# Adding the forget gates' running sums by the score product, as rows beside the keys' low halves

## The chip, the cores and the metric

The kernel runs on one core of a Trainium2 chip. The metric is the device time of one execution in microseconds (us). Three runs of the kernel before gave 1219.63, 1219.83 and 1220.3 us; the median is 1219.83.

## What is computed

Two layers, each of an attention part and a feed-forward part, over 512 tokens of 1024 numbers. The attention part has three groups of four heads: "fox" (a causal softmax with a bias from forget gates), "diff" (two score maps a head) and "mla". The change is in the fox heads:

```python
def fox_group(q, k, v, f_logit, f_bias):          # 4 heads of 64
    logf = log_sigmoid(f_logit + f_bias)
    cum = cumsum(logf, axis=1).transpose(0, 2, 1)  # one running sum a head
    def bias(qi, ki):
        d = cum[query] - cum[key]
        return where(ki <= qi, d, -1e30)
    return softmax(q @ k.T * 64 ** -0.5 + bias) @ v
...
for each layer:
    h = rmsnorm(x) @ w_in          # split into q, k, v, gates of all heads
    x = x + concat(fox, diff, mla) @ w_o
    up = conv(rmsnorm(x) @ w_up);  x = x + (silu(g) * u) @ w_down
```

All is float32. The kernel keeps that precision by splitting a number into a high and a low half of TensorE's faster float type and multiplying three times (high by high, high by low, low by high).

## The kernel before, in words

Each layer has these stages. First, products that give tokens in rows: the gates and fox values (`w_fx`), then the diff values (`w_dv`), with two projections between (`fm(0)` and `fm(2)`, the first two fox queries and keys). Then the "weave": the twelve heads, two at a time, are interleaved with the remaining projections and with the output product, which fill TensorE while a head waits for its softmax. These fillers are the groups of `mm` products of 128x512. Last, the feed-forward part, nothing but large products.

A fox head keeps queries as one tile whose upper 64 partitions hold one head's high half and whose other 64 hold its low half. The keys are a tile `k` (the high half twice) and a tile `lo` (the low half in the head's own 64 partitions, zeros in the other 64). Scores are two products with the same `q`: `q` by `k`, then `q` by `lo`.

A head is a job of steps: four scores `s(3)`, `s(2)`, `s(1)`, `s(0)` of 512, 384, 256 and 128 columns, transposes `t(kt)` of the weight rows, and products `v(kt)` with the values into the tile `o`. `soft` is one VectorE instruction that adds the bias to the scores and takes the minimum (`nm`), then an exponential on ScalarE, then a reciprocal (`rsum`) on VectorE; `plain` scales the row on GpSimd; `transposed` turns the row on TensorE (tile `at`) and splits it into `ph` and `pl`.

The biases of a fox head come from `prep`. The running sums stand in `cum`, one column for each block and head. Four transposes by the identity (`at<-c_sb,cum`) spread a head's sums over all partitions, ScalarE copies them negated (`r`), VectorE makes the masked blocks (`r<-c_sb,at`), and GpSimd adds the query's own sum into four bias tiles `b` (seven instructions). Heads 0 and 1 do this before the weave, heads 2 and 3 as a step of heads 0 and 1, in line before `t(1)`.

The order on every engine is made when the program is built: a table of costs in `Plan` estimates when a tile is ready, `weave` takes a head's step if it is ready by then and a filler otherwise, and a scheduler below it orders each engine's own queue. Engines work in order, each through its own queue. All compute instructions carry one line of the program, L135 (a helper that records them), so groups are told apart by tile names.

Of the kernel before, what the change touches and what calls it, by code (L numbers as in the profile page):

```python
# [14 lines left out]
P = 128  # L15
# [19 lines left out]
NPAR = DEPTH * PL  # L35


C_ID, C_TRI, C_ONE, C_CAU, C_COS, C_SIN, C_MLA, C_ALI = 0, 128, 256, 384, 512, 576, 640, 1152
NCST = C_ALI + S

BIG = 3.0e38
HALVES = (slice(0, 64), slice(64, 128))
# [116 lines left out]
def constants():  # L159
    c = np.zeros((P, NCST), np.float32)  # L160
    p = np.arange(P)
    c[:, C_ID:C_ID + P] = np.eye(P)
    c[:, C_TRI:C_TRI + P] = np.where(p[:, None] <= p[None, :], 8.0, 0.0)
    c[:, C_ONE:C_ONE + P] = 8.0
    c[:, C_CAU:C_CAU + P] = np.where(p[None, :] <= p[:, None], 0.0, 8 * NEG)
# [12 lines left out]

def build(tc, xT, cst, par, lamv, w_fm, w_dv, w_fx, w_uq, w_ukv, w_o, w_o2, w_up, w_dn, w_dt, fin, out):
# [4 lines left out]
    with ctx:  # L184
# [23 lines left out]
        def U():  # L208
            return plan.tile("u", 2, up_.tile([P, S], F32, name="u", tag="u"))

        def B(qt):
            return plan.tile(f"b{qt}", 1, pp.tile([P, (qt + 1) * P], F32, name=f"b{qt}", tag=f"b{qt}"))
# [21 lines left out]
        g_sb = cp.tile([P, KD], F32, name="g_sb")  # L234
        par_sb = cp.tile([P, NPAR], F32, name="par_sb")
        mhalf = cp.tile([P, NT], F32, name="mhalf")
        ones = cp.tile([P, 2], F32, name="ones")

        nc.scalar.dma_start(g_sb, par[:, O_LN1:O_LN1 + KD])
# [1 line left out]
        nc.vector.memset(rest.bitcast(F32), 0.0)  # L241
        nc.gpsimd.memset(ones, 1.0)
        nc.gpsimd.memset(mhalf, -0.5)
        warm = small(2, "warm")
        nc.scalar.activation(warm, ones, AF.Copy)

# [224 lines left out]
                else:  # L471
                    assert not (jobs or side or fillers), "nothing can go on"

        def head_job(name, gates, maps, reads, bias_of, scale, v_mul, o_put, combine, prep=None):

            job = Job(name, gates)
            rows, pT, out = [None] * NT, {}, []

            def s(qt):
                def emit():  # L480
                    rs, ts = [], []
                    b = bias_of(qt)
                    for m in maps:
                        ps = m(qt)
                        t = row_tile(qt) if not ts else U()
                        rs.append(soft(ps, qt, t, b, scale))
                        ts.append(t)
                    combine(qt, ts, rs)
                    rows[qt] = ts[0]
                job.add(emit, lambda: (reads(), "sc"))  # L490

            def t(kt):
                def emit():
                    pT[kt] = transposed(rows, kt)
                job.add(emit, lambda: (rows[kt:], "at"))

            def v(kt):
                def emit():
# [6 lines left out]
            if prep:  # L505
                job.add(prep)
# [25 lines left out]
        def attention(l, norm):  # L532
# [19 lines left out]
            def stacked_queries(i, scale=1.0):  # L552

                yield from fm(i)
                t = got[i]
                got[i] = []
                for m in range(2):
                    q = A()
                    own, other = HALVES[m], HALVES[1 - m]
                    nc.scalar.activation(q[own], t[own], AF.Copy, scale=scale)  # L560
                    if scale == 1.0:
                        nc.vector.tensor_tensor(out=q[other], in0=t[own], in1=q[own].bitcast(F32), op=ALU.subtract)
                    else:
                        nc.vector.scalar_tensor_tensor(out=q[other], in0=t[own], scalar=scale, in1=q[own].bitcast(F32), op0=ALU.mult, op1=ALU.subtract)
                    got[i].append(q)
                yield f"fm{i}"

            def stacked_keys(i):

                yield from fm(i)  # L570
                t = got[i]
                got[i] = []
                for m in range(2):
                    k, lo = A(), A()
                    own, other = HALVES[m], HALVES[1 - m]
                    nc.gpsimd.memset(lo[other].bitcast(F32), 0.0)
# [3 lines left out]
                    got[i].append((k, lo))  # L580
                yield f"fm{i}"

            def stacked_tiles(iq, ik):
                return lambda: [*got[iq], *(t for pair in got[ik] for t in pair)]
# [41 lines left out]
            norm.spread()  # L626
            for _ in first:
                pass
            marks[f"fm{FM_ORDER[0]}"] = 0.0
# [9 lines left out]
            marks[f"fm{FM_ORDER[1]}"] = 0.0  # L639


            nz = NT * 4
# [16 lines left out]
            cum = small(nz, "cum")  # L659
            cum_ps = at_ps()  # L660

            def cumulate(k):
                if k != 5:
                    return
                nc.tensor.matmul(cum_ps[:, 0:nz], lhsT=c_sb[:, C_TRI:C_TRI + P], rhs=lf, start=True, stop=False)
                for t in range(1, NT):
                    nc.tensor.matmul(cum_ps[:, 4 * t:nz], lhsT=c_sb[:, C_ONE:C_ONE + P], rhs=lf[:, 0:nz - 4 * t], start=False, stop=t == NT - 1)
                nc.vector.tensor_copy(cum, cum_ps[:, 0:nz])

            def rotate(dst, src, cs, sn, shape, name):  # L670

# [18 lines left out]


            acc = tm(w_dv, S, (mm_ps, mm_ps, sc_ps, sc_ps), cumulate)
            dv = []
            for t in range(NT):
                dv.append(split(acc[t], scale=rs1[:, t:t + 1]))
# [101 lines left out]


            jobs = []
            box = {}  # L800
            preps = {}

            def plain(qt, ts, rs):
                n = (qt + 1) * P
# [26 lines left out]
            def fox(h):  # L831
                pair, par = divmod(h, 2)

                def bias(qt):
                    n = (qt + 1) * P
                    b = B(qt)
                    nck, msk = box[f"nck{h}"]
                    for src, c in ((nck, slice(0, n - P)), (msk, slice(n - P, n))):
                        if c.start < c.stop:
                            nc.gpsimd.tensor_scalar(out=b[:, c], in0=src[:, c], scalar1=1.0, scalar2=cum[:, 4 * qt + h:4 * qt + h + 1], op0=ALU.mult, op1=ALU.add)  # L840
                    box[f"b{h}_{qt}"] = b

                def prep():
                    ps = over_partitions([cum[:, 4 * t + h:4 * t + h + 1] for t in range(NT)])
                    nck, msk = R(), R()
                    nc.scalar.activation(nck, ps, AF.Copy, scale=-1.0)
                    for t in range(NT):
                        c = slice(t * P, (t + 1) * P)
                        nc.vector.tensor_tensor(out=msk[:, c], in0=c_sb[:, C_CAU:C_CAU + P], in1=ps[:, c], op=ALU.subtract)
                    box[f"nck{h}"] = nck, msk  # L850
                    for qt in reversed(range(NT)):
                        bias(qt)

                if h < 2:
                    prep()
                else:
                    preps[h - 2] = prep

                def bias_of(qt):
                    return box[f"b{h}_{qt}"]  # L860

                return head_job(f"fox{h}", [f"fm{pair}", f"fm{2 + pair}"],
                                [stacked_scores(pair, 2 + pair, par)], stacked_tiles(pair, 2 + pair), bias_of, 0.125,
                                halves_mul(lambda: fv, h), pair_put(f"f{pair}", par, pair), plain, lambda: preps[h]() if h in preps else None)

            def diff(h):
                def combine(qt, ts, rs):
# [217 lines left out]
```

## Time and profile before

| What | Before |
|---|---|
| median of three runs | 1219.83 us |
| the profiled execution, whole | 1220.15 us |
| its span, first to last instruction | 1218.3 us |
| granted TensorE clock, mean | 0.999 of full speed |
| TensorE busy | 1205.1 us (99%) |
| VectorE busy | 822.1 us (67%) |
| ScalarE busy | 661.9 us (54%) |
| GpSimd busy | 208.1 us (17%) |

TensorE's records overlap, so its cost is read from the distance between starts and not from the durations. The weave runs from about 54 to 260 us in the first layer and from about 654 to 860 us in the second; the two layers look alike.

### The profile page before, as it was taken

The numbers are of one execution on the slowest core, as the hardware profiler recorded it, in microseconds if no ns is written. First come the engines' busy times: TensorE is split into PE (matmuls) and PEld (weight loads), VectorE is DVE, ScalarE is ACT, GpSimd is POOL, SyncE is SP. The second block draws the span as 40 slices with busy tenths as digits, with TensorE's granted clock in tenths as the row PEclk, the third lists the DMA queues.
The fourth block names the chain that finished last, engine by engine and source line by source line (L and its number), as shares of the span: only waits on it lengthen the run. The fifth ranks groups of instructions, "written<-read, shape, count | busy, mean of one in ns | idle before, by whom it ended". The sixth has DMA issues, their size and how long they took to land.

```text
span 1218.3 us, 16462 instructions
## 1 busy us (share of the span) xinstructions
PE 1205.1 (99%) x5776; PEld 1005.2 (83%) x5776; DVE 822.1 (67%) x1691; ACT 661.9 (54%) x1323; POOL 208.1 (17%) x320
## 2 busy tenths in 40 slices
PE   9999999999999999999999999999999999999997
PEld 8888888888888888888888888888888888888886
DVE  6678888787674366765556888877767634676743
ACT  6577787555543245444455776866555422545424
POOL 0262432001110001010013415220111100101102
PEclk9999999999999999999999999999999999999999
DMA  6321111223323333223323211112332233232331
GB/s 230 113 70 48 57 53 40 88 86 105 103 81 86 113 103 103 99 72 95 90 101 104 70 66 49 40 49 88 100 102 100 72 100 112 102 100 91 102 106 69
DMA packets 34497, 108.31 MB, mean 89 GB/s; under 512 B 3952, under 2 KB 4080, under 8 KB 34416
## 3 DMA queue, kind: packets, MB, share of 16 engines
q1 hardware_dynamic: 33840, 106.45, 27.1%
q8 instruction: 45, 0.74, 0.3%
q10 hardware_dynamic: 576, 0.83, 0.2%
q14 instruction: 36, 0.29, 0.1%
HBM read 105.16 MB, written 2.10 MB: 88 GB/s over the span
## 4 chain that ended last, share of the span: by engine, by line
PE 93%; POOL 2%; DVE 2%; ACT 2%; issue 1%; DMA 0%; POOLq 0%; SPq 0%; ACTq 0%; DVEq 0%
PE mm L135 78%; PE sc L135 8%; PE at L135 4%; PE o L135 3%; POOL b L135 1%; DVE w L135 1%; ACT u L135 1%; ACT row L135 0%; POOL row L135 0%; DVE a L135 0%; DVE row L135 0%; DMA raw<-in_w_fx 0%; ACT a L135 0%; POOL rsd L135 0%; ACT w L135 0%
## 5 line engine op out<-in xcount | busy, mean ns | idle before, releaser
L135 PE MATMUL mm<-a,whi 128*128 128x512 f32 x2736 | 850.9, 392 | 0.0
L135 PEld LDWEIGHTS mm<-a,whi 128*128 128x128 f32 x2736 | 508.4, 188 | 101.8 <-DVE a L135 0.4
L135 PE MATMUL mm<-a,wlo 128*128 128x512 f32 x1368 | 533.2, 390 | 0.0
L135 ACT ACTIVATE whi<-raw 128x512 fp32r<-128x512 f32 (+3 forms) x426 | 248.0, 584 | 362.5 <-PE mm L135 323.8
L135 DVE TENSOR_TENSOR wlo<-raw,whi 128x512 fp32r<-128x512 f32 (+3 forms) x426 | 272.8, 641 | 126.8 <-ACT whi L135 122.0
L135 PEld LDWEIGHTS mm<-a,wlo 128*128 128x128 f32 x1368 | 256.8, 188 | 53.5
L135 DVE SCALAR_TENSOR_TENSOR w<-u,par_sb,w 128x510 f32<-128x510 f32 (+1 forms) x176 | 133.0, 761 | 28.0 <-ACT w L135 25.3
L135 POOL TENSOR_TENSOR a<-w,a 128x512 fp32r<-128x512 f32 x44 | 57.6, 1309 | 527.4 <-ACT a L135 508.1
L135 DVE TENSOR_TENSOR u<-mm,r 128x512 f32<-128x512 f32 x84 | 58.0, 691 | 98.9 <-PE mm L135 98.9
L135 ACT ACTIVATE a<-w 64x512 fp32r<-64x512 f32 (+1 forms) x124 | 78.3, 631 | 40.9 <-DVE w L135 39.5
L135 ACT ACTIVATE w<-u,par_sb 128x512 f32<-128x512 f32 x88 | 71.4, 815 | 29.4 <-DVE u L135 29.3
L135 POOL TENSOR_SCALAR row<-row,rsum 128x512 f32<-128x512 f32 (+1 forms) x96 | 57.4, 600 | 151.8 <-DVE rsum L135 144.1
L135 PE MATMUL sc<-a 128*128 128x512 f32 (+7 forms) x288 | 66.5, 338 | 1.6 <-DVE nm L135 1.6
L135 DVE TENSOR_TENSOR x<-mm,x 128x512 f32<-128x512 f32 x64 | 43.9, 688 | 34.0 <-PE mm L135 33.7
L135 ACT ACTIVATE row<-row,nm 128x512 f32<-128x512 f32 (+1 forms) x96 | 53.8, 561 | 18.3 <-DVE nm L135 17.9
L135 PEld LDWEIGHTS sc<-a 128*128 128x128 f32 (+1 forms) x288 | 45.4, 190 | 7.2 <-DVE nm L135 3.0
L135 DVE TENSOR_TENSOR pl<-at,ph 128x128 fp32r<-128x128 f32 (+1 forms) x96 | 45.7, 482 | 7.5 <-ACT ph L135 7.1
L135 ACT ACTIVATE ph<-at 128x128 fp32r<-128x128 f32 (+1 forms) x96 | 40.8, 433 | 14.0 <-PE at L135 8.7
L135 PE MATMUL mm<-whi,a 128*128 128x512 f32 (+2 forms) x144 | 46.7, 363 | 0.0
L135 PE MATMUL at<-c_sb,row 128*128 128x128 f32 x240 | 42.1, 276 | 0.9 <-POOL row L135 0.9
L135 POOL TENSOR_SCALAR b<-r,cum 128x128 f32<-128x128 f32 (+2 forms) x56 | 28.8, 527 | 63.4 <-ACT r L135 42.9
L135 ACT ACTIVATE w<-w 128x512 f32<-128x512 f32 x50 | 31.7, 634 | 14.4 <-DVE w L135 11.5
(156 smaller groups left out, 1072.9 us busy)
## 6 DMA issues: line engine op xcount, KB each, us to landing
raw<-in_w_up SPq DMA_DIRECT2D x88, 512.0 KB, 3.3
raw<-in_w_fm SPq DMA_DIRECT2D x30, 512.0 KB, 3.2
raw<-in_w_dn SPq DMA_DIRECT2D x24, 384.0 KB, 3.1
raw<-in_w_dn SPq DMA_DIRECT2D x24, 320.0 KB, 2.9
raw<-in_w_o SPq DMA_DIRECT2D x16, 384.0 KB, 3.1
raw<-in_w_dv SPq DMA_DIRECT2D x8, 512.0 KB, 3.3
raw<-in_w_dn SPq DMA_DIRECT2D x8, 512.0 KB, 3.5
raw<-in_w_o SPq DMA_DIRECT2D x4, 512.0 KB, 3.3
```

The costliest lines, as they stand in the source:

```text
L135: return real(*args, **kw)
```

## The change

The sums are no longer biases. `cumulate`, which runs inside the `w_dv` product, splits the sums into high and low halves of four heads (`hl`, eight numbers a token and block); GpSimd copies them into a mostly zero tile `gate_rows` at four places, and two steps later four transposes turn it, and ScalarE copies the result to `box["sums"]`, in which partitions now hold sums and columns hold tokens. `summed` writes such rows into the half of a 64-partition pair that held nothing: for keys into the zeros beside the low half in `lo`, with a minus sign and rows of ones; for queries into a new tile `q2`, whose other half is a copy of `q`'s. The second score product now is `q2` by `lo`, so the 64 idle rows of the product add the sums. The bias that `soft` adds is the constant causal mask.

```diff
+            def summed(i):
+                for m in range(2):
+                    own, other = HALVES[m], HALVES[1 - m]
+                    if i < 2:
+                        q = got[i][m]
+                        out, f = A(), C_SUM + 2 + 2 * (2 * i + m)
+                        nc.gpsimd.tensor_copy(out[own], q[own])
+                        got[i][m] = q, out
+                    else:
+                        out, f = got[i][m][1], C_SUM
+                    nc.gpsimd.tensor_scalar(out=out[other], in0=box["sums"][other], scalar1=c_sb[other, f:f + 1], scalar2=c_sb[other, f + 1:f + 2], op0=ALU.mult, op1=ALU.add)
...
+                    nc.tensor.matmul(ps[:, :n], lhsT=q[:, c], rhs=k[:, :n], start=True, stop=False)
+                    nc.tensor.matmul(ps[:, :n], lhsT=q2[:, c], rhs=lo[:, :n], start=False, stop=True)
...
             def cumulate(k):
+                if k == 7:
+                    ps = at_ps()
+                    for t in range(NT):
+                        nc.tensor.transpose(ps[:, t * P:(t + 1) * P], in_=gate_rows[:, t, :], identity=ident)
+                    box["sums"] = R()
+                    nc.scalar.activation(box["sums"], ps, AF.Copy)
                 if k != 5:
                     return
...
-                nc.vector.tensor_copy(cum, cum_ps[:, 0:nz])
+                nc.scalar.activation(hl[:, :, 0:4], src, AF.Copy)
+                nc.vector.tensor_tensor(out=hl[:, :, 4:8], in0=src, in1=hl[:, :, 0:4].bitcast(F32), op=ALU.subtract)
+                for c in (0, 8, 64, 72):
+                    nc.gpsimd.tensor_copy(gate_rows[:, :, c:c + 8], hl.bitcast(F32))
...
             acc = tm(w_dv, S, (mm_ps, mm_ps, sc_ps, sc_ps), cumulate)
+            for i in FM_ORDER[:2]:
+                summed(i)
...
-                def prep():
-                    ps = over_partitions([cum[:, 4 * t + h:4 * t + h + 1] for t in range(NT)])
-                    nck, msk = R(), R()
-                    nc.scalar.activation(nck, ps, AF.Copy, scale=-1.0)
-                    for t in range(NT):
-                        c = slice(t * P, (t + 1) * P)
-                        nc.vector.tensor_tensor(out=msk[:, c], in0=c_sb[:, C_CAU:C_CAU + P], in1=ps[:, c], op=ALU.subtract)
-                    box[f"nck{h}"] = nck, msk
-                    for qt in reversed(range(NT)):
-                        bias(qt)
```

`fm(1)` and `fm(3)` call `summed` at their ends; the zeroing of `lo` goes for fox keys; the table of constants grows from 1664 to 2058 columns.

The order moves with it. On TensorE, at the end of the `w_dv` product of the first layer and the start of the weave, `sc` being score tiles, `mm` the products and `at` the transposes, before:

```order
L135 MATMUL sc<-whi,a 128x512
L135 MATMUL at<-c_sb,cum 128x128 x8
L135 MATMUL mm<-a,whi 128x512 x2
L135 MATMUL mm<-a,wlo 128x512
...
L135 MATMUL mm<-a,whi 128x512 x2
L135 MATMUL mm<-a,wlo 128x512
L135 MATMUL sc<-a 128x512 x2
L135 MATMUL sc<-a 128x384 x2
```

And now, from the last twelve products of `w_dv` on:

```order
L137 MATMUL sc<-whi,a 128x512
L137 MATMUL at<-c_sb,gate_rows 128x128 x4
L137 MATMUL mm<-whi,a 128x512
...
L137 MATMUL mm<-a,whi 128x512 x2
L137 MATMUL mm<-a,wlo 128x512
L137 MATMUL sc<-a 128x512 x2
L137 MATMUL sc<-a 128x384 x2
```

The eight transposes after `w_dv` are gone, four stand twelve products before its end, and the first scores come after 18 filler products of 512 columns instead of 12.

On TensorE further on, between the last score of head 0 (128 columns) and the transpose of the row that it gives (`row_862` before, `row_858` now), before:

```order
L135 MATMUL sc<-a 128x128 x2
L135 MATMUL mm<-a,whi 128x512
L135 MATMUL at<-c_sb,cum 128x128 x4
L135 MATMUL mm<-a,whi 128x512
L135 MATMUL mm<-a,wlo 128x512
...
L135 MATMUL at<-c_sb,row_751 128x128
L135 MATMUL at<-c_sb,row_862 128x128
```

And now:

```order
L137 MATMUL sc<-a 128x128 x2
L137 MATMUL mm<-a,whi 128x512 x2
L137 MATMUL mm<-a,wlo 128x512
...
L137 MATMUL at<-c_sb,row_790 128x128
L137 MATMUL sc<-a 128x256 x2
L137 MATMUL mm<-a,whi 128x512 x2
...
L137 MATMUL at<-c_sb,row_858 128x128
```

The four transposes of the sums are gone, and 30 filler products stand between the two places instead of 12.

On GpSimd, from the weave's start on, where `b` are bias tiles, `r` the spread sums and `row` the softmax rows, before:

```order
L135 TENSOR_SCALAR b_721<-r,cum 128x128
L135 TENSOR_SCALAR row_751<-row_751,rsum 128x512
L135 TENSOR_SCALAR row_762<-row_762,rsum 128x384
L135 MEMSET a 64x512
L135 TENSOR_SCALAR row_789<-row_789,rsum 128x512
L135 TENSOR_SCALAR row_800<-row_800,rsum 128x384
L135 TENSOR_SCALAR b_724<-r,cum 128x128 x2
L135 TENSOR_SCALAR b_727<-r,cum 128x128
L135 TENSOR_SCALAR row_844<-row_844,rsum 128x256
L135 TENSOR_SCALAR b_882<-r,cum 128x384
L135 TENSOR_SCALAR b_885<-r,cum 128x256
L135 TENSOR_SCALAR row_862<-row_862,rsum 128x128
```

And now:

```order
L137 COPY a<-a 64x512 x2
L137 COPY gate_rows<-hl 128x4x8 x4
L137 TENSOR_SCALAR a<-r,c_sb 64x512 x4
L137 TENSOR_SCALAR row_735<-row_735,rsum 128x512
L137 TENSOR_SCALAR row_746<-row_746,rsum 128x384
L137 TENSOR_SCALAR a<-r,c_sb 64x512
L137 COPY a<-a 64x512 x2
L137 TENSOR_SCALAR a<-r,c_sb 64x512
L137 TENSOR_SCALAR row_790<-row_790,rsum 128x512
L137 TENSOR_SCALAR row_801<-row_801,rsum 128x384
L137 TENSOR_SCALAR a<-r,c_sb 64x512
L137 TENSOR_SCALAR row_840<-row_840,rsum 128x256
```

The `b` instructions between the rows are gone; fewer and wider ones that write the sums' rows stand between them, and none is left once `fm(3)` is done.

## Rows read from the trace of the kernel before

**Rows 1.** The page, busy time of the engines.

```profile
PE 1205.1 (99%) x5776; PEld 1005.2 (83%) x5776; DVE 822.1 (67%) x1691; ACT 661.9 (54%) x1323; POOL 208.1 (17%) x320
```

**Rows 2.** Waits of PE: line, waited for, us in total, times, longest.

```profile
PE sc L135 <- DVE nm L135: 1.6, 2, 0.8
...
PE at L135 <- POOL row L135: 0.9, 2, 0.4
PE at L135 <- DVE pl L135: 0.8, 2, 0.4
```

**Rows 3.** The chain of waits in time order: start, us, work.

```profile
89.99 4.13 PE mm L135 x18
```

**Rows 4.** Timeline of PE, heads 0 and 1: start, us, instruction, [idle before].

```profile
54.11 1.04 PE L135 MATMUL at<-c_sb,cum 128*128 128x128 f32 x8
54.90 0.70 PE L135 MATMUL mm<-a,whi 128*128 128x512 f32 x2
55.45 0.40 PE L135 MATMUL mm<-a,wlo 128*128 128x512 f32 x1
```

**Rows 5.** Timeline of PE, the sums of head 2.

```profile
65.58 0.44 PE L135 MATMUL mm<-a,whi 128*128 128x512 f32 x1
66.15 0.65 PE L135 MATMUL at<-c_sb,cum 128*128 128x128 f32 x4
66.56 0.48 PE L135 MATMUL mm<-a,whi 128*128 128x512 f32 x1
66.87 0.39 PE L135 MATMUL mm<-a,wlo 128*128 128x512 f32 x1
```

**Rows 6.** Timeline of PE, the sums of head 3.

```profile
76.68 0.62 PE L135 MATMUL at<-c_sb,cum 128*128 128x128 f32 x4
77.06 0.71 PE L135 MATMUL sc<-a 128*128 128x512 f32 x2
```

**Rows 7.** Timeline of PE, four transposes between products of another stage.

```profile
25.43 0.65 PE L135 MATMUL at<-c_sb,rsn 128*128 128x128 f32 x4
25.84 0.71 PE L135 MATMUL mm<-a,whi 128*128 128x512 f32 x2
26.39 0.40 PE L135 MATMUL mm<-a,wlo 128*128 128x512 f32 x1
```

**Rows 8.** Timeline of VectorE and PE around the running sums.

```profile
46.00 0.17 DVE L135 COPY cum<-at 128x16 f32<-128x16 f32 x1 [2.10 <-PE at L135]
...
51.39 0.39 PE L135 MATMUL mm<-whi,a 128*128 128x512 f32 x1
```

**Rows 9.** Groups by form: instruction, shapes, count, busy us, mean ns, idle before.

```profile
L135 POOL TENSOR_TENSOR a<-w,a 128x512 fp32r<-128x512 f32 x44 | 57.6, 1309 | 527.4 <-ACT a L135 508.1 <-issue 19.3
...
L135 POOL TENSOR_SCALAR row<-row,rsum 128x512 f32<-128x512 f32 x24 | 18.5, 771 | 43.8 <-DVE rsum L135 43.8
...
L135 POOL TENSOR_TENSOR rsn<-vn,mhalf 128x4 f32<-128x4 f32 x4 | 4.1, 1016 | 166.7 <-DVE vn L135 166.7
...
L135 POOL COPY w<-krr 128x128 f32<-128x128 f32 x8 | 2.2, 291 | 7.4 <-DVE a L135 7.4
```

**Rows 10.** The same groups, ScalarE.

```profile
L135 ACT ACTIVATE whi<-raw 128x512 fp32r<-128x512 f32 x278 | 174.5, 630 | 231.4 <-PE mm L135 194.0 <-PE sc L135 29.7 <-issue 1.9
```

**Rows 11.** The bias tiles' instructions: count, ns min/median/max, first and last start, forms.

```profile
L135 POOL TENSOR_SCALAR b<-r,cum x56: 370/380/990, 56.1 to 691.9; 128x128 f32<-128x128 f32 x40, 128x384 f32<-128x384 f32 x8, 128x256 f32<-128x256 f32 x8
```

**Rows 12.** Timeline of PE and GpSimd, the row of head 0's last score.

```profile
69.19 0.49 PE L135 MATMUL at<-c_sb,row 128*128 128x128 f32 x3
...
69.68 0.37 POOL L135 TENSOR_SCALAR row<-row,rsum 128x128 f32<-128x128 f32 x1
...
70.10 0.66 PE L135 MATMUL at<-c_sb,row 128*128 128x128 f32 x4 [0.43 <-POOL row L135]
```

**Rows 13.** Weight loads of one layer's score products: count, ns min/median/max, first and last start, forms.

```profile
L135 PEld LDWEIGHTS sc<-a x144: 186/190/212, 57.5 to 220.7; 128*128 128x128 f32 x96, 96*128 96x128 f32 x48
```

**Rows 14.** Windows: stretch, its us, busy us of PE, PEld, DVE, ACT, POOL, clock, DMA.

```profile
165.00:205.00 40.00, 39.39 (x232) 31.46 (x231) 35.97 (x109) 33.80 (x99) 9.59 (x17) 1.00 0.08 27
```

More of the change, by code (lines that the diff above doesn't have):

```diff
@@ L35 @@
 NPAR = DEPTH * PL
-C_ID, C_TRI, C_ONE, C_CAU, C_COS, C_SIN, C_MLA, C_ALI = 0, 128, 256, 384, 512, 576, 640, 1152
-NCST = C_ALI + S
+C_ID, C_TRI, C_ONE, C_COS, C_SIN, C_MLA, C_ALI, C_CAU = 0, 128, 256, 384, 448, 512, 1024, 1536
+C_SUM = C_CAU + S
+NCST = C_SUM + 10
 BIG = 3.0e38
@@ L164, in constants @@
     c[:, C_ONE:C_ONE + P] = 8.0
-    c[:, C_CAU:C_CAU + P] = np.where(p[None, :] <= p[:, None], 0.0, 8 * NEG)
+    c[:, C_CAU + S - P:C_CAU + S] = np.where(p[None, :] <= p[:, None], 0.0, 8 * NEG)
+    row = p % 64
+    first, second = row < 8, (row >= 8) & (row < 16)
+    c[:, C_SUM], c[:, C_SUM + 1] = -1.0 * first, second
+    for h in range(FOX_H):
+        own = row % FOX_H == h
+        c[:, C_SUM + 2 + 2 * h], c[:, C_SUM + 3 + 2 * h] = second & own, first & own
     half = ROPE // 2
@@ L209, in U @@
             return plan.tile("u", 2, up_.tile([P, S], F32, name="u", tag="u"))
-        def B(qt):
-            return plan.tile(f"b{qt}", 1, pp.tile([P, (qt + 1) * P], F32, name=f"b{qt}", tag=f"b{qt}"))
         def R():
@@ L236, in build @@
         mhalf = cp.tile([P, NT], F32, name="mhalf")
+        gate_rows = cp.tile([P, NT, P], F32, name="gate_rows")
         ones = cp.tile([P, 2], F32, name="ones")
@@ L243, in build @@
         nc.gpsimd.memset(mhalf, -0.5)
+        nc.gpsimd.memset(gate_rows, 0.0)
         warm = small(2, "warm")
@@ L472, in weave, with head_job @@
                     assert not (jobs or side or fillers), "nothing can go on"
-        def head_job(name, gates, maps, reads, bias_of, scale, v_mul, o_put, combine, prep=None):
+        def head_job(name, gates, maps, reads, bias_of, scale, v_mul, o_put, combine):
             job = Job(name, gates)
@@ L504, in head_job @@
             s(3), s(2), t(3), s(1), t(2), s(0)
-            if prep:
-                job.add(prep)
             t(1), t(0)
@@ L565, in stacked_queries @@
                     got[i].append(q)
+                if i == 1:
+                    summed(i)
                 yield f"fm{i}"
@@ L575, in stacked_keys @@
                     own, other = HALVES[m], HALVES[1 - m]
-                    nc.gpsimd.memset(lo[other].bitcast(F32), 0.0)
+                    if i >= 4:
+                        nc.gpsimd.memset(lo[other].bitcast(F32), 0.0)
                     nc.scalar.activation(k[own], t[own], AF.Copy)
@@ L580, in stacked_keys, with summed_tiles, summed_scores, f @@
                     got[i].append((k, lo))
+                if i == 3:
+                    summed(i)
                 yield f"fm{i}"
+            def summed(i):
[9 more added lines that the diff above has]
+                    nc.gpsimd.tensor_scalar(out=out[other], in0=box["sums"][other], scalar1=c_sb[other, f:f + 1], scalar2=c_sb[other, f + 1:f + 2], op0=ALU.mult, op1=ALU.add)
+            def summed_tiles(iq, ik):
+                return lambda: [t for i in (iq, ik) for pair in got[i] for t in pair]
+            def summed_scores(iq, ik, m):
+                def f(qt):
+                    n = (qt + 1) * P
+                    (q, q2), (k, lo) = got[iq][m], got[ik][m]
+                    c = slice(qt * P, n)
+                    ps = sc_ps()
+                    nc.tensor.matmul(ps[:, :n], lhsT=q[:, c], rhs=k[:, :n], start=True, stop=False)
+                    nc.tensor.matmul(ps[:, :n], lhsT=q2[:, c], rhs=lo[:, :n], start=False, stop=True)
+                    return ps
+                return f
             def stacked_tiles(iq, ik):
@@ L628, in attention @@
                 pass
-            marks[f"fm{FM_ORDER[0]}"] = 0.0
             rs1 = norm.rs
@@ L638, in attention @@
                 pass
-            marks[f"fm{FM_ORDER[1]}"] = 0.0
             nz = NT * 4
@@ L657, in attention @@
             nc.vector.scalar_tensor_tensor(out=lf, in0=z, scalar=0.0, in1=ln, op0=ALU.min, op1=ALU.subtract)
-            cum = small(nz, "cum")
+            box = {}
             cum_ps = at_ps()
             def cumulate(k):
+                if k == 7:
[4 more added lines that the diff above has]
+                    nc.scalar.activation(box["sums"], ps, AF.Copy)
                 if k != 5:
@@ L667, in cumulate @@
                     nc.tensor.matmul(cum_ps[:, 4 * t:nz], lhsT=c_sb[:, C_ONE:C_ONE + P], rhs=lf[:, 0:nz - 4 * t], start=False, stop=t == NT - 1)
-                nc.vector.tensor_copy(cum, cum_ps[:, 0:nz])
+                src = cum_ps[:, 0:nz].rearrange("p (t h) -> p t h", t=NT)
+                hl = sp.tile([P, NT, 8], F32R, name="hl", tag="hl", bufs=1)
+                nc.scalar.activation(hl[:, :, 0:4], src, AF.Copy)
+                nc.vector.tensor_tensor(out=hl[:, :, 4:8], in0=src, in1=hl[:, :, 0:4].bitcast(F32), op=ALU.subtract)
+                for c in (0, 8, 64, 72):
+                    nc.gpsimd.tensor_copy(gate_rows[:, :, c:c + 8], hl.bitcast(F32))
             def rotate(dst, src, cs, sn, shape, name):
@@ L692, in attention @@
             acc = tm(w_dv, S, (mm_ps, mm_ps, sc_ps, sc_ps), cumulate)
+            for i in FM_ORDER[:2]:
+                summed(i)
+                marks[f"fm{i}"] = 0.0
             dv = []
@@ L799, in attention @@
             jobs = []
-            box = {}
-            preps = {}
             def plain(qt, ts, rs):
@@ L832, in fox @@
                 pair, par = divmod(h, 2)
[L834 to L841, printed above, removed]
-                def prep():
-                    ps = over_partitions([cum[:, 4 * t + h:4 * t + h + 1] for t in range(NT)])
-                    nck, msk = R(), R()
-                    nc.scalar.activation(nck, ps, AF.Copy, scale=-1.0)
-                    for t in range(NT):
-                        c = slice(t * P, (t + 1) * P)
-                        nc.vector.tensor_tensor(out=msk[:, c], in0=c_sb[:, C_CAU:C_CAU + P], in1=ps[:, c], op=ALU.subtract)
-                    box[f"nck{h}"] = nck, msk
-                    for qt in reversed(range(NT)):
-                        bias(qt)
[L854 to L860, printed above, removed]
                 return head_job(f"fox{h}", [f"fm{pair}", f"fm{2 + pair}"],
-                                [stacked_scores(pair, 2 + pair, par)], stacked_tiles(pair, 2 + pair), bias_of, 0.125,
-                                halves_mul(lambda: fv, h), pair_put(f"f{pair}", par, pair), plain, lambda: preps[h]() if h in preps else None)
+                                [summed_scores(pair, 2 + pair, par)], summed_tiles(pair, 2 + pair),
+                                lambda qt: c_sb[:, C_CAU + S - (qt + 1) * P:C_CAU + S], 0.125,
+                                halves_mul(lambda: fv, h), pair_put(f"f{pair}", par, pair), plain)
             def diff(h):
```

## The prediction

> **What bounds the kernel now.** I read the page first. TensorE is busy 99% of the span and the next engine 67% [rows 1]: a microsecond taken from TensorE's own list of work is a microsecond of the whole, and one taken from another engine is worth only what TensorE waits for that engine. The waits of PE say how little that is: 0.9 us for normalised rows, 1.6 for `nm` and 0.8 for `pl`, each in two pieces, one for each layer [rows 2]. Then the chain of waits gives the pace of undisturbed products: 18 of 512 columns in 4.13 us, 0.229 us each [rows 3]. Last comes the timeline of PE at the places that the change touches. There the reader is to look at the distance between starts, not at durations.
>
> **What leaves TensorE.** In each layer three groups of transposes of `cum` go.
> - The eight for heads 0 and 1 take 54.90 - 54.11 = 0.79 us, and the first two products after them 0.55 where 0.46 is the pace: 0.88 in all [rows 3, 4].
> - The four for head 2 take 66.56 - 66.15 = 0.41, the product after them 0.31 instead of 0.23: 0.49. Before them a product that should take 0.23 lasts 0.57, because the group waits for `pl` to free its tile, so 0.34 more goes [rows 2, 5]. What is late next there is the transposes of head 0's rows; they come below.
> - The four for head 3 take 0.38 [rows 6].
>
> That is 2.09 us a layer. The new four transposes are priced by four others between the same kinds of product: 25.84 - 25.43 = 0.41, and 0.55 instead of 0.46 for the next two products: 0.50 [rows 7]. Net 1.59 a layer, 3.2 us in two layers.
>
> **The score product** gets another weight tile for its second half. Today one tile serves both, so a saved load might be feared lost. But a layer's weave has 32 score products for fox, 64 for diff and 48 for mla, 144, and 144 loads stand there: each product loads its own already [rows 13]. The idle rows of the array that now carry the sums cost no columns. Nothing is added.
>
> **The new wait inside `w_dv`.** Behind the new transposes stand the last twelve products of `w_dv`, in line and with no filler, so every microsecond they are late is lost. Their input: the sums are in PSUM at 46.00, where VectorE copies them in 0.17 [rows 8]. Now ScalarE makes the high half and VectorE the low half, each about as short (0.2); both may stand behind a weight split (0.63 on ScalarE, about as long on VectorE) [rows 10]; then four small copies on GpSimd. A copy of 128 columns takes 0.29 and the slowest small instruction there 1.02 [rows 9], so four take 1.2 to 4.1. They end between 46.0 + 0.4 + 1.2 = 47.6 and 46.0 + 0.4 + 1.3 + 4.1 = 51.8; the transposes are reached at 51.39 [rows 8]. I take the copies' price, near 48 to 49, and nothing; at the other end it is 0.4 us a layer.
>
> **The rows before the first scores.** Transposes end near 51.8; ScalarE may be in a weight split of 0.63, then copies the sums in about the same, so GpSimd starts near 53.1 [rows 10]. Head 0 needs the first and third of four instructions of 512 columns. The nearest is the scaling of a row, 0.77 [rows 9]; the shortest bias instruction is 0.37 and the longest 0.99 where the median is 0.38, a delay of 0.62 [rows 11], so 0.37 to 1.39 each. Three end between 54.2 and 57.3, at 55.4 by the row's price. `w_dv` ends at 54.1 + 0.5, and 18 filler products of 0.229 put the first scores at 58.7. Hidden at either end. One shape takes 0.37 and at times 0.99 there [rows 11]. The Trainium skill, "SBUF — State Buffer", section "Who interferes with whom", says that a VectorE instruction with both inputs in SBUF and a GpSimd one that reads SBUF lock each other out for a whole instruction. Weight splits are such instructions, and the spread agrees: by this rule alone the new rows would sit at their upper price, and the sum here stays, since 57.3 is before 58.7.
>
> **GpSimd, VectorE, ScalarE.** In a layer 28 bias instructions and four clearings go; eight rows (0.77) and four copies of 512 columns come (from 0.29 to 1.31, the two-input form of that width; I take 0.6) with the four small ones [rows 9, 11]. GpSimd's queue in the fox stretch is lighter. VectorE loses sixteen masked blocks, ScalarE three copies for one small one. All this is hidden behind TensorE and worth nothing by itself, except at one place. The transposes of head 0's rows start at 69.19, and the next at 70.10, 0.9 later; three transposes are 0.3, so 0.6 is waiting, and it ends on GpSimd's row at 69.68 [rows 12], which stood behind bias instructions. These go, and 30 products instead of 12 stand between the score and that transpose. The wait may come back at a later row, behind the new instructions: I count half of it, 0.3 a layer, 0.6 in all; the ends are 1.2 and nothing. The larger constant table lands before its first use and costs nothing.
>
> **The sum.** 3.2 + 0.6 = 3.8 us off the profiled execution's 1220.15 is 1216.35. The median of the runs shown stands 0.32 below that execution, so the forecast is **1216.0 us**. What a measurement of this kernel can tell from no change is about 0.2%, 2.4 us: faster means below 1217.4, slower above 1222.3.
>
> **Rivals.**
> - *The other waits go too.* The row waits vanish wholly (1.2), and so do the 1.6 us for `nm` [rows 2], at the last fox score, since VectorE has less to do there and the order around it changes. 3.2 + 1.2 + 1.6 = 6.0: 1213.8 us. For it: both waits are in the stretch that is relieved. Against: a new order on four engines seldom removes waits without making some.
> - *GpSimd's new rows become the wait.* The rows of `fm(1)` and `fm(3)` stand among the rows of heads 0 and 1. Two rows and two copies at 1.39 and 1.31 are 5.4 us in line, at low prices 2.1; if half of the 3.3 between is not covered, 1.65 a layer eats the 1.59: 1219.9, no change. For it: the spread in [rows 11] and today's wait in [rows 12]. Against: the fillers between are more than doubled.
> - *The end of the weave starves*, the one that ends slower. The order spends fillers earlier: before the first value product of diff head 0 stand 270 filler products instead of 246, before that of mla head 0 408 in both. So 24 fewer, 5.5 us a layer, cover the same softmax work between. VectorE is busy 36.0 of the 40 us at the end of this stretch, 4.0 idle [rows 14]: if that idle time absorbed all it can, 1.5 would be lost, if nothing, 5.5. The middle, 3.5 a layer, gives 7.0 - 3.2 = 3.8 more: 1223.6. It decides from 1.6 a layer (no gain) and is slower from 2.8. Against it: the 35 us before are less tight, and the estimates that order the steps held there until now.
>
> **Chances.** Forecast 0.52, with its own range 1214.8 to 1217.6; all waits gone 0.20; GpSimd 0.14; starving 0.14, of which 0.05 above 1222.3, 0.07 between and 0.02 below. Faster: 0.49 of the first, all of the second, 0.02 of the last, 0.71. Slower 0.05. Same the rest, 0.24. The range leaves out the end of the second case below and most of the last above: 1213.4 to 1219.6.
>
> **What would show it.** Right: eight transposes from `gate_rows` and none from `cum`; 24 fewer products on PE; no idle time of PE at the new transposes or at the first scores; the copies `gate_rows<-hl` done some 2 us before; in the fox stretch PE's wait for `row` smaller. Wrong: PE waiting for GpSimd's `a` at a score or at the new transposes; waits of PE for `nm`, `pl` or `row` between 130 and 205 us that together exceed those of before by 1.6 us a layer; a GpSimd row of 64x512 far above 1.39 us.

## The result, and the profile after

The changed kernel takes 1228.96 us (median of 6, 1227.82 to 1229.9) against 1220.26 for the kernel before (median of 6): ratio 1.0071, 95% interval 1.0061 to 1.0082. It is slower by 8.7 us; the forecast was 1216.0.

The page after, busy time of the engines in us (PE is TensorE, PEld its weight loads, DVE VectorE, ACT ScalarE, POOL GpSimd), answers to [rows 1]:

```profile
PE 1207.6 (98%) x5752; PEld 1006.5 (82%) x5752; DVE 820.0 (67%) x1659; ACT 658.0 (54%) x1319; POOL 199.2 (16%) x289
```

24 instructions of PE are gone, as foreseen, and the other engines have less to do. Yet the span is 1227.5 us instead of 1218.3: what came is waiting and, as the windows below show, a stretch at a lower clock. The waits of PE (engine, tile, what it waited for: us in total, times, longest) against [rows 2]:

```profile
PE sc L137 <- DVE nm L137: 6.0, 4, 2.8
PE at L137 <- DVE pl L137: 2.0, 4, 0.9
```

Before, the score's wait for `nm` was 1.6 us in two pieces; now there are four pieces, two of them of 2.8, one in each layer. The timeline of PE at the first (start, us, instruction, count, [idle before]):

```profile
165.97 0.64 PE L137 MATMUL sc<-a 128*128 128x128 f32 x4
169.37 0.71 PE L137 MATMUL sc<-a 128*128 128x512 f32 x2 [2.76 <-DVE nm L137]
169.97 0.41 PE L137 MATMUL at<-c_sb,row 128*128 128x128 f32 x2
...
171.39 1.05 PE L137 MATMUL mm<-a,whi 128*128 128x512 f32 x2
172.24 0.63 PE L137 MATMUL mm<-a,wlo 128*128 128x512 f32 x1
```

The first line is the last score `s(0)` of diff head 2, the second the first score of diff head 3, with no filler between. The last two lines show a second loss: two products of 512 columns take 0.85 us from start to start (171.39 to 172.24), 0.43 each, where the pace is 0.23. The windows (stretch, its us, PE busy, granted clock, DMA share, GB/s) show why:

```profile
166.00:169.50 3.50, 0.74 (x7) 1.00 0.00 0
169.50:174.00 4.50, 4.47 (x14) 0.67 0.01 4
174.00:180.00 6.00, 6.00 (x36) 0.97 0.00 0
```

And within them, with the columns of all engines (busy PE, PEld, DVE, ACT, POOL, then the clock):

```profile
172.50:173.00 0.50, 0.50 (x2) 0.40 (x2) 0.50 (x2) 0.50 (x3) 0.38 (x1) 0.50 0.00 0
```

Behind the wait TensorE is granted its lower level, 1.2 instead of 2.4 GHz, for most of 4.5 us; the kernel before has 1.00 in the same windows.

What it means for the order is seen in the number of filler products (tile `mm`) that PE has done when a head's step comes. The windows of PE's `mm` instructions in layer 1, each up to one step: diff head 0's first value product, diff head 2's first score and its last score, mla head 1's first value product. (The last is the step that the prediction calls mla head 0's: 408 products stand before head 1's in both kernels, before head 0's, at 197.97 and 205.61 us, 380 and 394.) Before:

```profile
54.00:134.01 80.01, 61.30 (x246) 1.00 0.19 65
54.00:145.41 91.41, 68.33 (x276) 1.00 0.18 60
54.00:161.94 107.94, 79.77 (x324) 1.00 0.19 62
...
54.00:208.04 154.04, 103.31 (x408) 1.00 0.17 54
```

And after, up to the same four steps:

```profile
54.00:138.71 84.71, 66.10 (x270) 1.00 0.20 64
54.00:153.82 99.82, 77.25 (x318) 1.00 0.19 63
54.00:165.97 111.97, 84.39 (x345) 1.00 0.19 63
...
54.00:212.43 158.43, 104.67 (x408) 0.99 0.16 52
```

The diff heads come 24, 42 and 21 products later in the list than before. At diff head 2's last score 345 of the 408 are used up, and 63 are left up to the fourth step instead of 84.

### The profile page after: what moved, and what is told of

Its sections match the earlier page's. It is cut to its first block, busy times and chain, and to the rows that moved or that the text cites. A ratio compares the mean times of both kernels' runs of the same rounds, so it can differ in the third digit from the quotient of the medians.

```text
span 1227.5 us, 16378 instructions
## 1 busy us (share of the span) xinstructions
PE 1207.6 (98%) x5752; PEld 1006.5 (82%) x5752; DVE 820.0 (67%) x1659; ACT 658.0 (54%) x1319; POOL 199.2 (16%) x289
## 4 chain that ended last, share of the span: by engine, by line
PE 89%; DVE 4%; ACT 4%; POOL 1%; issue 1%; DMA 0%; POOLq 0%; SPq 0%; DVEq 0%; ACTq 0%
PE mm L137 76%; PE sc L137 7%; PE at L137 4%; PE o L137 2%; DVE w L137 1%; ACT a L137 1%; DVE a L137 1%; DVE row L137 1%; ACT u L137 1%; ACT row L137 1%; DVE pl L137 1%; POOL rq L137 0%; POOL row L137 0%; DVE wlo L137 0%; ACT ph L137 0%
## 5 line engine op out<-in xcount | busy, mean ns | idle before, releaser
L137 ACT ACTIVATE a<-w 64x512 fp32r<-64x512 f32 (+1 forms) x124 | 78.2, 631 | 46.5 <-DVE w L137 44.8
L137 POOL TENSOR_SCALAR row<-row,rsum 128x512 f32<-128x512 f32 (+2 forms) x96 | 57.9, 605 | 199.8 <-DVE rsum L137 186.7
L137 ACT ACTIVATE row<-row,nm 128x512 f32<-128x512 f32 (+2 forms) x96 | 53.7, 560 | 27.9 <-DVE nm L137 27.8
L137 PEld LDWEIGHTS sc<-a 128*128 128x128 f32 (+1 forms) x288 | 46.3, 190 | 11.8 <-ACT a L137 5.7
L137 DVE TENSOR_TENSOR pl<-at,ph 128x128 fp32r<-128x128 f32 (+2 forms) x96 | 45.9, 483 | 7.5 <-ACT ph L137 6.9
L137 DVE CUSTOM_DVE_ANT_0 row<-sc,c_sb 128x512 f32<-128x512 f32 (+2 forms) x96 | 45.3, 483 | 5.0 <-PE sc L137 4.4
L137 ACT ACTIVATE ph<-at 128x128 fp32r<-128x128 f32 (+2 forms) x96 | 41.0, 433 | 13.3 <-PE at L137 10.7
L137 PEld LDWEIGHTS at<-c_sb,row 128*128 128x128 f32 x240 | 28.8, 141 | 15.2 <-issue 4.3
```

The costliest lines, as they stand in the source:

```text
L137: return real(*args, **kw)
```

## The experiments

Twelve kernels ran. Medians are given with the kernel before of the same chip, ratios with their 95% interval.

| Kernel | us | before | ratio |
|---|---|---|---|
| 1 new work, old order | 1217.74 | 1220.19 | 0.9983 (0.9974 to 0.9992) |
| 2 old work, new order | 1231.13 | 1220.19 | 1.0096 (1.0080 to 1.0111) |
| 3 score queued behind | 1230.03 | 1220.19 | 1.0086 (1.0072 to 1.0100) |
| 4 wait filled | 1228.64 | 1220.19 | 1.0071 (1.0059 to 1.0084) |
| 5 new fox order, old diff order | 1218.58 | 1220.24 | 0.9987 (0.9978 to 0.9995) |
| 6 old fox order, new diff order | 1229.21 | 1220.24 | 1.0071 (1.0059 to 1.0084) |
| 7 slack 1.25 | 1220.87 | 1220.24 | 1.0007 (0.9998 to 1.0016) |
| 8 slack 1.0 | 1219.08 | 1220.24 | 0.9994 (0.9985 to 1.0003) |
| 9 rows on ScalarE | 1218.08 | 1219.81 | 0.9987 (0.9978 to 0.9995) |
| 10 the same, filler first | 1216.84 | 1219.81 | 0.9979 (0.9970 to 0.9989) |
| 11 rows later | 1216.06 | 1219.80 | 0.9973 (0.9963 to 0.9983) |
| 12 the same, filler first | 1214.82 | 1219.80 | 0.9961 (0.9948 to 0.9974) |

### Work and order apart (1 and 2)

The weave takes its steps from a written list: a letter is a step of a head, a dot a filler. Experiment 1 gives the new work the list of before, 2 the old work the new list.

```diff
-                if best and (best[0] <= plan.pe + SLACK or not step):
-                    best[1].step(marks)
...
+            for c in ORDER:
+                if c != ".":
+                    named[c].step(marks)
```

> The changed kernel's work with the steps of the heads and the fillers taken in the order in which the kernel before took them (its prep steps left out). Theory A (the change's own work saves about 3.2 us of TensorE, and the loss of 8.7 us comes from the new order of the weave, above all from the 2.8 us wait before the first score of diff head 3 in each layer and the half granted clock behind it): 1216.0 to 1218.0 us, no PE wait above 1 us between 130 and 205 us, granted clock 1.0 there. Theory B (the new instructions themselves, GpSimd's rows and copies or the second query tile, hold up the engines): 1226 to 1229 us, whatever the order.

> The work of the kernel before (biases from transposes) with the steps of the heads and the fillers in the changed kernel's order, each prep step put right behind the 128-column score of its head as before. Theory A: the order brings the loss with it, 1220.3 + 12 = about 1232 us (1229 to 1234), with a wait of 2 to 3 us before diff head 3's first score in each layer and a granted clock near half behind it. Theory B: 1219 to 1222 us, no such wait.

The new work on the old order is 2.45 us faster than before, the old work on the new order 10.9 slower; together 8.5, and the change made 8.7. Theory B falls: the loss is the order's, whichever work it carries. In experiment 2 the wait is there too:

```profile
PE sc L140 <- DVE nm L140: 6.9, 6, 2.8
```

### Is it the wait, or the clock behind it? (3 and 4)

Experiment 3 queues the waiting score behind the last product of the mla keys; experiment 4 fills the wait with twelve products that nobody reads.

```diff
+                    with tc.issue_after(box["last"]):
+                        return f(qt)
```

> The changed kernel with one edge more: the first score of diff head 3 is queued on TensorE behind the last product of the mla keys, so that two transposes of rows and three products of 512 columns (0.2 + 0.7 us) that stood behind the waiting score now stand ahead of it. If that score was only put too early on TensorE (theory A in its narrow form): the wait falls from 2.8 to about 1.9 us in each layer, 1.8 us less in all, 1227; and if the shorter wait leaves the granted clock at full, 3.4 us less on top, 1223.6 us. Rival: VectorE is the limit there in any case, and what is won before the score is lost behind it: 1228.5 to 1229.5 us.

```diff
+                    spare = op_.tile([P, S], F32, name="o", tag="o")
...
+                            for _ in range(FILL):
+                                tc.nc.tensor.matmul(spare, lhsT=q[:, 0:P], rhs=q, start=True, stop=True)
```

> The changed kernel with twelve products of 128x512 into an unused tile right ahead of the first score of diff head 3 in each layer, 12 x 0.227 = 2.7 us of work that nobody reads, in the time in which TensorE waits. If the granted clock falls there because TensorE had nothing to do: it stays at 1.0, the products behind the score take 0.23 instead of 0.43 us each, and 1.7 us a layer come back, 1225.5 us (1225 to 1226.5). Rival (the clock falls there for another reason, and the wait alone makes the loss): 1229 to 1230 us with the granted clock near 0.65 in the 4 us behind the score.

In experiment 3 the long wait of the score is gone, but the transposes that now stand ahead of it wait for VectorE's `a` (the split of a turned mla query tile, which frees an `at` tile), and longer. The time is 1230.0, no gain, as the rival had it and a little above its range. Timeline of PE:

```profile
166.27 0.64 PE L137 MATMUL sc<-a 128*128 128x128 f32 x4
170.26 0.41 PE L137 MATMUL at<-c_sb,row 128*128 128x128 f32 x2 [3.35 <-DVE a L137]
```

In experiment 4 the products fill the wait and the clock stays at 1.00 (windows as above), yet only 0.3 us are won, not 3.4, and that is within the noise: the time lies between the two ranges of the expectation. Timeline of PE:

```profile
165.25 0.64 PE L138 MATMUL sc<-a 128*128 128x128 f32 x4
165.73 2.94 PE L902 MATMUL o<-a 128*128 128x512 f32 x12
168.66 0.70 PE L138 MATMUL sc<-a 128*128 128x512 f32 x2
...
171.67 0.55 PE L138 MATMUL at<-c_sb,row 128*128 128x128 f32 x3 [0.78 <-ACT u L138]
...
174.56 0.62 PE L138 MATMUL at<-c_sb,rsd 128*128 128x128 f32 x4 [0.77 <-DVE pl L138]
```

```profile
164.50:169.00 4.50, 4.50 (x25) 1.00 0.01 4
169.00:173.50 4.50, 3.37 (x17) 1.00 0.00 0
```

TensorE, no longer slowed, waits 0.8 us for ScalarE and 0.8 for VectorE instead, and 0.7 in smaller pieces further on. So neither the one wait nor the clock is the cause: they are the form that the loss takes in the changed kernel. The price is read from the stretch between diff head 2's last score and mla head 1's first value product (window, its us, busy PE, PEld, DVE, ACT, POOL, clock). The first line is the kernel before, then in fences of their own the changed kernel, experiment 1 and experiment 4:

```profile
161.94:208.04 46.10, 45.49 (x265) 36.58 (x263) 40.53 (x126) 37.42 (x111) 13.11 (x25) 1.00 0.12 36
```

```profile
165.97:212.43 46.46, 42.55 (x239) 34.17 (x238) 37.33 (x120) 36.94 (x114) 12.67 (x21) 0.96 0.08 26
```

```profile
160.38:206.58 46.20, 45.59 (x264) 36.54 (x263) 40.58 (x127) 37.41 (x112) 13.28 (x25) 1.00 0.11 35
```

```profile
165.25:211.88 46.63, 44.23 (x254) 34.82 (x252) 38.98 (x127) 37.16 (x116) 13.33 (x22) 1.00 0.08 26
```

It takes 46.1 to 46.6 us with 84 fillers in it or with 63, at full clock or with a part of it at the lower one, with the wait empty or filled. Other runs agree: experiment 6, also with 63 fillers, takes 46.45 us, and only with 90, as in experiment 8, is the stretch longer:

```profile
165.76:212.21 46.45, 42.53 (x240) 34.15 (x238) 37.31 (x120) 36.94 (x114) 12.67 (x21) 0.96 0.08 26
```

```profile
157.24:205.20 47.96, 46.58 (x268) 37.98 (x267) 40.28 (x126) 38.67 (x118) 15.04 (x26) 1.00 0.10 31
```

So the kernel before had, it seems, about as many fillers as the stretch has room for. With 63 TensorE's work no longer sets its length: TensorE waits for the softmaxes of diff heads 2 and 3 and the transposes between. That this chain of steps sets it is inferred. It is not a chain of softmaxes alone: the chain of waits through the stretch of the changed kernel runs for some 31 of the 46.5 us on TensorE, 13 of them in `mm` products that stand between the steps, and for 13 on the other engines (35 and 11 in the kernel before). Which link could be shorter was not tried. What the order loses is then the 21 products done before the stretch instead of in it: 21 x 0.229 [rows 3] = 4.8 us a layer. From experiment 1 to the changed kernel the stretch begins 165.97 - 160.38 = 5.6 us later and is 0.3 longer, 5.9 in the first layer; at the stretch's end in the second layer the changed kernel is 817.14 - 805.72 = 11.4 us behind, of the 11.8 by which the spans differ. Of the 0.8 that the 21 products leave of the 5.6, 0.6 stood there before the weave began (its first filler starts at 54.82 us against 54.25), and four transposes of an mla tile (162.63 to 162.98) now stand ahead of the stretch instead of in it.

### Where the order goes wrong (5 to 8)

The list is cut where the fox heads end, behind its first 84 characters. Experiment 5 takes the new list up to there and before's list from there on, experiment 6 before's list and then the new one.

> The changed kernel's work; its own order of steps for the fox heads (the first 84 steps of the weave), the order of the kernel before from there on. The number of filler products of 512 columns that TensorE has done before a step: 18, 96, 114 and 174 at the first scores and value products of the fox heads as in the changed kernel, but 246 at diff head 0's first value product, 276 at diff head 2's first score, 354 at its first value product, as before (270, 318, 364 in the changed kernel). Theory D (the loss is made in the diff heads, which come later against the fillers, so that these are used up while diff heads 2 and 3 are still in their softmaxes): 1216.5 to 1218.5 us. Rival F (it is made in the fox heads, whose softmaxes are spread thinner): 1226 to 1229 us.

> The other half: the changed kernel's work, the fox heads in the order of the kernel before, the diff heads in the changed kernel's order (180 products at fox head 3's first value product, then 270, 318, 364 as in the changed kernel). Theory D: 1228 to 1230 us, with the wait of 2 to 3 us before diff head 3's first score. Rival F: 1217 to 1219 us.

Theory D holds for both: the new fox order costs nothing clear of the noise (1218.58, 0.1 above its range, against 1217.74 in experiment 1), the new diff order all of it (1229.21, with the waits of 2.8 us).

```diff
-WIDTH, SLACK = 2, -1.5
+WIDTH, SLACK = 2, -1.25
```

> The changed kernel with one number changed: the planner takes a step of a head if its estimate says that it is ready 1.25 us before TensorE is free, instead of 1.5. The heads then run ahead of the fillers as before: 12 products before the first scores (18 in the changed kernel), 246 at diff head 0's first value product, 276 at diff head 2's first score, 354 at its first value product. Theory D: 1216.5 to 1218.5 us, and no wait above 1 us at diff head 3's first score. If the new order owes its loss to something else than these counts: above 1222 us.

> The same number at 1.0 us: heads earlier still (78 products at fox head 0's first value product, 246 at diff head 0's, 276 at diff head 2's first score, 348 at its first value product, 380 at mla head 0's first score). Theory D: as much as with 1.25 or less, 1215.5 to 1218.5 us. Against it works that a step taken 0.25 us closer to its estimate waits where the estimate is short: if ten such waits of 0.3 us a layer come, 1222 us.

One number of the planner brings the counts back (246 at diff head 0's first value product and 276 at diff head 2's first score, as before), and 8 and 10 us of the loss with them. But 7 missed its range by 2.4 us and 8 by 0.6. The long wait is gone; many small ones stand in its place. PE's waits in experiment 7:

```profile
PE at L137 <- DVE pl L137: 3.3, 10, 0.4
PE at L137 <- DVE row L137: 1.5, 2, 0.8
```

Before, `pl` was 0.8 [rows 2]. The counts explain the large loss, not these.

### What was left of the forecast (1, 9 and 11)

Experiment 1 won 2.45 us, not 3.8. The waits of PE there:

```profile
PE at L142 <- POOL row L142: 1.6, 2, 0.8
```

This is the wait of [rows 12], of which half was to go: it was 0.9 us in all [rows 2] and is 1.6. The timelines of GpSimd and VectorE just before it, in experiment 1:

```profile
62.33 1.63 POOL L142 CAST a<-a 64x512 fp32r<-64x512 f32 x2
64.07 1.08 POOL L142 TENSOR_SCALAR a<-r,c_sb 64x512 fp32r<-64x512 f32 x1
65.14 0.69 POOL L142 TENSOR_SCALAR row<-row,rsum 128x512 f32<-128x512 f32 x1
```

```profile
62.52 1.99 DVE L142 TENSOR_TENSOR a<-w,a 64x512 fp32r<-64x512 f32 x2
...
64.62 1.74 DVE L142 TENSOR_TENSOR wlo<-raw,whi 128x512 fp32r<-128x512 f32 x1
...
66.36 0.40 DVE L142 CUSTOM_DVE_ANT_0 row<-sc,c_sb 128x256 f32<-128x256 f32 x1
```

While GpSimd makes the last of the new rows of heads 2 and 3 and, right behind it, scales a softmax row, VectorE's weight split lasts 1.74 us, and the score row that the transposes need stands behind it.

```diff
+                    if i % 2:
+                        nc.scalar.activation(out[other], box["sums"][other], AF.Identity, scale=c_sb[other, f:f + 1], bias=c_sb[other, f + 1:f + 2])
+                        continue
```

> The changed work in the order of the kernel before, and the rows and query copies that are made inside the weave (two rows for keys, two rows and two copies for queries, of 64x512, in each layer) made by ScalarE instead of GpSimd; TensorE's order is the same as in the first experiment. There GpSimd's row of 64x512 at 64.07 took 1.08 us, VectorE's weight split at 64.62 took 1.74 us where 0.67 is usual, and TensorE waited 0.97 us at 67.39 for the normalised row that came behind. Theory L (VectorE was held while GpSimd's new instruction ran): the split takes 0.67 again, the wait falls to 0.3 us or less, 1.3 us less in all, 1216.4 us. Rival (six more instructions of 0.63 us on ScalarE hold up the exponentials of fox heads 0 and 1 as much): 1217.5 to 1219 us, with TensorE waiting for ScalarE there.

With the rows on ScalarE, VectorE's split takes 0.67 again, but the rows now stand ahead of the exponentials, and a wait for `row` of 0.6 us a layer is left:

```profile
PE at L142 <- POOL row L142: 1.1, 2, 0.6
```

```profile
64.22 0.67 DVE L142 TENSOR_TENSOR wlo<-raw,whi 128x512 fp32r<-128x512 f32 x1
```

The time, 1.7 below before, doesn't differ from experiment 1's beyond the intervals. The rival was right on the time, theory L on the split.

```diff
-                    summed(i)
+                    late.append(lambda: summed(i))
...
+                        with tc.issue_after(scaled[0]):
```

> The changed work in the order of the kernel before, TensorE's order as in the first experiment; the four rows and two query copies of 64x512 of fox heads 2 and 3 stay on GpSimd, but are queued there behind the last row of fox head 0 (from about 68.3 us) instead of between the rows of heads 0 and 1 (61.5 to 65.1). Moved to ScalarE they had only changed one wait for another (0.97 to 0.71 us). Theory L (what made the wait is that they held VectorE and stood ahead of rows that TensorE needs sooner): VectorE's split at 64.6 takes 0.67 instead of 1.74 us, the wait at 67.4 falls to 0.3 us or less, 1.3 us less than in the first experiment in all, 3.7 below the kernel before: 1216.4 us. Rival: six instructions of 0.9 us end near 73.7, and the first score of head 2, due at 75.5, waits for the one that is last, or the holding of VectorE only moves to 69 to 74 us: 1217.5 to 1218.5 us.

Here the six instructions stay on GpSimd, behind head 0's last row. VectorE and PE at the same place:

```profile
64.12 0.67 DVE L142 TENSOR_TENSOR wlo<-raw,whi 128x512 fp32r<-128x512 f32 x1
```

```profile
67.48 0.40 PE L142 MATMUL mm<-a,wlo 128*128 128x512 f32 x1
67.72 0.93 PE L142 MATMUL at<-c_sb,row 128*128 128x128 f32 x7
```

The split takes 0.67 us and the wait is gone, as theory L had it. The time is 3.74 us below before: what the prediction's sum gave for the change, though the wait went whole and not by half as the sum had it. The ratio's interval overlaps experiment 1's, so the 1.3 us between the two medians are an estimate; that the split and the wait changed is seen in the traces.

### One filler earlier (10 and 12)

A part of the list, before and after:

```diff
-cccccddde...de
+cccccddd.e..de
```

> The same, and two filler steps of three products each put ahead of diff head 0's first score instead of behind it, where TensorE waits 0.93 us for VectorE's nm at 104 us in the kernel before and in the first experiment alike. If that wait is only a matter of one step that comes too early: it goes, 0.9 us less in each layer than without it, 1214.6 us. Rival: diff head 0 is later by these products (0.7 to 1.4 us) and the wait comes back behind, where the fillers end: 1216 to 1217.5 us.

> The same with the two filler steps ahead of diff head 0's first score, which took a wait of 0.93 us out of each layer when the rows were on ScalarE: another 1.2 to 1.8 us less, 1215 us, 5 below the kernel before. If the two edits share one slack and don't add up: 1216.4 to 1217 us.

The dot that moves is six products. It takes away the 0.8 us wait of diff head 0's first score, and the median falls by 1.24 us in both (9 to 10: 1218.08 to 1216.84; 11 to 12: 1216.06 to 1214.82), two thirds of the 1.8 hoped for; the intervals within each pair overlap. Experiment 10's time lies in its rival's range although the wait is gone, 12's is as expected. The last version beats both kernels: 5.0 us under the one before and, by the two ratios, some 13.5 under the changed one. PE's waits there:

```profile
PE o L142 <- DVE a L142: 1.4, 1, 1.4
PE at L142 <- DVE pl L142: 0.8, 2, 0.4
```

## Why the prediction was wrong

- **What leaves TensorE: right.** Timeline of PE after, the new transposes, against [rows 4 to 7]:

```profile
51.62 0.60 PE L137 MATMUL at<-c_sb,gate_rows 128*128 128x128 f32 x4
51.97 0.48 PE L137 MATMUL mm<-whi,a 128*128 128x512 f32 x1
```

They take 0.35 us where 0.41 was counted. Experiment 11's 3.74 us are in line with the 3.2 counted here and a row wait that goes.

- **The wait in `w_dv` and the rows before the first scores: right**, both hidden. GpSimd after:

```profile
47.06 0.66 POOL L137 COPY gate_rows<-hl 128x32 f32<-128x32 f32 x4 [10.15 <-DVE hl L137]
53.12 3.84 POOL L137 TENSOR_SCALAR a<-r,c_sb 64x512 fp32r<-64x512 f32 x4 [5.41 <-ACT r L137]
```

The copies end a little before the 48 to 49 taken, four rows take 0.96 each where 0.77 was taken; three end at 56.0, the first scores start at 58.9.

- **The row wait: not tested by the changed kernel alone.** In its order the wait vanished. In the old order it grew from 0.9 to 1.6 us instead of losing 0.6, while VectorE's split was held up beside GpSimd's rows; it went when the new rows stood elsewhere. The prediction had the spread in [rows 11] and the sentence of the Trainium skill, "SBUF — State Buffer", section "Who interferes with whom": a VectorE instruction with both inputs in SBUF and a GpSimd one that reads SBUF exclude each other. The trace agrees (1.74 against 0.67 us). The prediction weighed it only for the rows before the first scores, where it changes nothing, and not for VectorE's splits inside the weave, where it cost some 1.3 us of the 3.8.

- **The step that failed: the sum counted the new order as free.** The loss is the third rival, "the end of the weave starves". Its mechanism and sign were right: 24 fewer fillers over the same softmax work. Two things in it were wrong. Its price: VectorE's idle 4.0 us [rows 14] was to absorb part, so that 1.5 to 5.5 us a layer would be lost, 3.5 in the middle. Between the two steps that it names, 24 fillers apart, the kernel before takes 208.04 - 134.01 = 74.03 us and the changed one 212.43 - 138.71 = 73.72: 5.5 us of products have gone from between them, and it is only 0.3 shorter. The 10.9 us in two layers of experiment 2, 5.5 a layer, are the upper end. VectorE's idle time was no reserve here: in the stretch VectorE is busy 37.3 of 46.5 us after and 40.5 of 46.1 before, so its work was not what set the length. And its chance, 0.14: the argument against it, that the planner's estimates "held there until now", says nothing of a new order, which those estimates had made by the same rule and which was already known to spend the fillers earlier. The forecast should have carried that count as a term of its sum. The sign that it gave for being wrong did come: between 165 and 213 us PE waits 3.0 us for `nm` where the kernel before waits 0.4 for `pl`. The half clock was not foreseen; experiment 4 gives it back and wins nothing clear of the noise.

- **The other rivals.** Not all waits went: `nm` is still waited for 1.5 us in experiment 11. A wait for GpSimd's `row` grew most where the fox heads kept the order of before and the new rows stood between theirs: to 1.6 us in experiment 1 and 2.0 in experiment 6.

## What to carry to other kernels

Where fillers hide the waits of a chain, count how many stand before each step of the chain in the new order: an edit that saves work can shift that count, and here every filler spent before the stretch that the chain sets was lost at nearly its full price. Test the work and the order apart, by replaying the old list of steps with the new work: the two effects here were -2.45 and +10.9 us, and the changed kernel shows only their sum. A wait with a slow clock behind it, however visible, is the price only if filling it makes the kernel faster.

## What the runs showed of the hardware

TensorE's granted clock fell to its lower level behind a wait of 2.76 us (2.75 in the second layer), and 512-column products took 0.43 instead of 0.23 us; with the wait filled it stayed at 1.00. The wait of 0.9 us for `pl` in the same kernel left it at 1.00. With GpSimd at work on a tile of 64x512 and then on a softmax row of 128x512, a VectorE split of 128x512 took 1.74 us instead of 0.67, and beside GpSimd's copies two of 64x512 took 1.99 instead of 1.40 (experiments 1 and 11).
